# Hybrid retention and attention layer on one core: where four waits at stage borders sit, and an order written out by hand

## The chip, the cores and the metric

The kernel runs on one core of a Trainium2 chip. A core has five engines that run their own instruction queues side by side: TensorE (PE, matrix products into PSUM; PEld is its weight load), VectorE (DVE), ScalarE (ACT), GpSimd (POOL) and SyncE (SP, which here only issues DMAs). They wait for each other through semaphores. The metric is device microseconds of one execution; lower is better. A profiled execution gives the trace, with times counted from the start of its span.

## What is computed

One layer of a diffusion backbone, batch 1: 1024 latent tokens of width 1024 and 256 context tokens. All is fp32. Cut to what matters here:

```python
h_lat = rms_norm(x, norm1_g) * (1 + sc1) + sh1              # scale and shift from c @ w_mod
# one input projection: retention q, k, v, gate | attention q, k, v
(rq, rk, rv, rg), (dq, dk, dv) = split_heads(h_lat @ w_in, rope_r, rope_d)   # and the same for ctx
# retention, 4 heads, both directions, chunks of 128:
S = S * c_dec + einsum('jd,je->de', kc * k_dec, vc)         # state carried from chunk to chunk
o = (qc @ kc.T * intra) @ vc + (qc * q_dec) @ S
y_ret = silu(rg) * (group_norm(o_forward) + group_norm(o_backward))
# differential attention, 4 heads, 1024 queries, 1280 keys:
a = softmax(q1 @ k1.T) - lam * softmax(q2 @ k2.T)
y_diff = rms_norm(a @ v) * g
x = x + g1 * (concat(y_ret, y_diff) @ w_out)
# gated MLP with a depthwise convolution of width 3 along the tokens:
u = conv3(h2 @ w_up); a, b = split(u)
x = x + g2 * ((silu(a) * b) @ w_down);  out = rms_norm(x) * final_g
```

## The kernel before

**Products in three passes.** Every large product splits both operands into a high and a low part (a ScalarE copy makes the high, a VectorE subtraction the low) and adds three products of 128x512 in `passes` (L129 to L134). A block of 512 output columns for 128 rows is 24 such products.

**Stages.** Modulation and first norm; the seven column blocks of the input projection, streamed in four slices of 512 KB each by `stream_block` (L213); retention, whose steps are generators that `tick` (L387) advances by a rate for each contraction step of a projection that runs at the same time (`beside`, L393); attention; output projection; the MLP, whose products are combined by a Strassen-like scheme over blocks j of columns; the down projection with the last norm.

**Who sets the order.** A planner that simulates the engines orders each engine's instructions, from the order in which the code emits them, their dependencies and the reuse of memory by tile pools. `in_order(start, engines)` (L120) pins the instructions emitted since `start` to the emitted order on the named engines. SP and POOL queues are in order as planned: a DMA that has to wait holds all behind it.

**The retention states.** `states_before` (L326) is a generator. Its first step emits three loads `kvgb` (L232); its second emits the first state product `pub` (L347, L348). At L854 the slices of block 3 are loaded, and at L855 the generator is put beside the gate projection `pn` (L856) at 36 steps in 62 ticks; a tick is three products.

**From queries to attention.** The queries are projected by `transposed` (L466) in blocks (head, half) of 24 products `pl`; `rotated` (L438) turns each: ScalarE swaps quarters of 32 partitions into `xb` (four times L443), VectorE forms `xa` (L446, L447, L448), `split_store` makes `xhl` (L434, L435) and SP stores it to `dq` (L436). The last two blocks are emitted at L992, after the first eight operations of attention unit 0 (`EARLY`, L990).

An attention unit is 128 queries of one head, 32 in all. Its operations are named by letters (L66): S scores (two maps, six products each into three PSUM banks, L890), M least value (L893, VectorE), E exponential with its sum (L897, ScalarE), R and C the weighted difference of both maps (L901, L902, L905, VectorE), T and K transposes and their copies in three groups `aT` (L910, L916), V value products (L922), O, Q copy and square (with `e` on GpSimd, L933), f the factor (VectorE L936, GpSimd power L937, kept as `pool_ins`), n, Y, h, l the scaled and turned result. Each map has one PSUM tile, so S of the next unit waits for E of this one. The loop over n at L1031 emits them in the order of `TAU` and pins it at L1051. The tiles `aT` lie in memory that the rotation's tiles had before.

**The MLP's first blocks.** L1390 to L1435 are an order by hand, pinned on PE, DVE and ACT. `multiplied` (L1380) is a VectorE product and, for an even block, a difference (L1273). `seventh_out` (L1333) copies a PSUM bank on ScalarE and adds the bank `fifth` on VectorE (L1335); that bank is then used again by the product `third` (L1360).

**The end.** `finished(r)` (L1648) scales the right half of rows r on ScalarE, stores it from SP (L1650), and `scaled` (L1570) does the left half on VectorE and stores it from SP (L1573).

Of the kernel before, what the change touches and what calls it, by code (L numbers as in the profile page):

```python
# [8 lines left out]
F32 = mybir.dt.float32  # L9
F32R = mybir.dt.float32r  # L10
# [7 lines left out]
P = 128  # L18
# [43 lines left out]
SPARE = (16, 4)  # L62
MOD_TICKS = 7
FIRST_LOADS = (22, 23, 25, 26, 28, 30)
EARLY = ("S1", "M1", "S0", "M0", "E1", "E0", "R", "C")
# [5 lines left out]
def r32(ap):  # L71
    return ap.bitcast(F32)
# [3 lines left out]
def kernel(  # L76
# [52 lines left out]
    def passes(ps, lt, rt, first, last, more=False):  # L129
        lh, ll = lt  # L130
        rh, rl = rt
        mm(ps, lh, rh, start=first, stop=False, skip_group_check=more)  # L132
        mm(ps, lh, rl, start=False, stop=False, skip_group_check=more)  # L133
        mm(ps, ll, rh, start=False, stop=last, skip_group_check=more)  # L134
# [21 lines left out]
    with ExitStack() as p1:  # L156
# [169 lines left out]
        def states_before():  # L326
            seq = [(h, c) for h in range(H) for c in (1, 0) + tuple(range(9, 2, -1))]
            pairs = [(h, c // 2) for h, c in seq if c % 2]
            waiting = []

            def ask():
                if pairs:
                    waiting.append(load_kvg(*pairs.pop(0), "b", ROW_KB, 2, bufs=5))

            kv = ahead = prev = Sb = None
            for _ in range(3):
                ask()
            for h, c in seq + [(None, None)]:
                cur = ahead
                if c is not None:  # L340
                    if c % 2:
                        kv = waiting.pop(0)
                        ask()
                    ahead = h, c, kv[:, 0, c % 2, :], kv[:, 1, c % 2, :]
                if cur is not None:
                    hc, cc, kk, v = cur
                    pu = pst.tile([P, P], F32, name="pub", tag="tr")  # L347
                    mm(pu, kk, v, start=True, stop=True)  # L348
# [502 lines left out]
        rtx = p1.enter_context(ExitStack())  # L851
        sb = rtx.enter_context(tc.tile_pool(name="sb", bufs=H - 1, side="right", reuse_waits="tile"))
        rt = rtx.enter_context(tc.tile_pool(name="rt", bufs=2, side="right", reuse_waits="tile"))
        wg = stream_block(3)  # L854
        beside(states_before(), 36 / 62)  # L855
        natural(wg, lat_lhs, range(NT), store_to(kvg_row(ROW_G), func=AF.Silu, c0=NTC))  # L856
        wg = stream_block(6)
        beside(outputs(), 1.05, -12.0)
# [10 lines left out]
        def loads(name, bufs=1, **kw):  # L869
            return aload.enter_context(tc.tile_pool(name=name, bufs=bufs, side="right", reuse_waits="tile", **kw))  # L870

        aq0, ak0, av, aq1, al, ak1 = (loads(*args) for args in (("aq0",), ("ak0",), ("av", 2), ("aq1",), ("al", 2), ("ak1",)))
        pss = {m: loads(f"pss{m}", space=PSUM) for m in (1, 0)}
        n_units = NT * H
        units = {}

        class Unit:
            def __init__(self, i):
                self.h, self.qt = divmod(i, NT)
# [31 lines left out]

            def turned(self, g):
                if self.aT is None:
                    self.aT = at.tile([P, NKT, P], F32, name="aT")
                n = min(4, NKT - 4 * g)
                nc.scalar.copy(self.aT[:, 4 * g : 4 * g + n, :], self.pt[g][:, :n, :])  # L916

# [41 lines left out]
        def load(i):  # L959
            h, qt = divmod(i, NT)  # L960
            ms = ((1, 2), (0, 1)) if i == 0 else ((0, 2),)
            behind = iter(FIRST_LOADS if i == 0 else ())

            def spaced():
                n = next(behind, None)
                return nullcontext() if n is None else tc.issue_after(steps[n].pool_ins)
            if qt == 0:
                cur["k"] = (ak0, ak1)[h % 2].tile([P, 2, LK], F32R, name="ks")
# [16 lines left out]
        warm = al.tile([P, 64], F32, name="warm", bufs=1)  # L985
        nc.scalar.activation(warm[:, 0:1], nlam, AF.Exp)
        fore = [load(i) for i in range(3)]
        units[0] = Unit(0)
        vars(units[0]).update(fore[0])
        for op in EARLY:  # L990
            units[0].run(op)
        transposed(wg, dq_d, rtab, 32, -DIFF_SCALE, 0, by_head[-TAIL:])  # L992
        psl.close()

    ctx_ya = ctx.enter_context(ExitStack())
# [27 lines left out]


    with ExitStack() as p2:
        at = p2.enter_context(tc.tile_pool(name="at", bufs=2, reuse_waits="tile"))
        psa = p2.enter_context(tc.tile_pool(name="psa", bufs=1, space=PSUM, reuse_waits="tile"))

        start = len(nc.cur_bb.bb.instructions)
        order = sorted(TAU.items(), key=lambda it: it[1] % 1.0)  # L1030
        for n in range(n_units + 8):  # L1031
            if 0 < n < n_units:
                units[n] = Unit(n)
                vars(units[n]).update(fore[n])
            if n == 9:
                with tc.issue_after(units[n - 5].pool_ins.ins):
                    nc.gpsimd.dma_start(out=g1, in_=g1_d)
            if n in (8, 10, 12, 14):
                a, i = divmod(n // 2 - 4, 2)
                with tc.issue_after(units[n - 5].pool_ins.ins):  # L1040
                    nc.gpsimd.dma_start(out=yT[a][i][:, 0:H, :], in_=yr_d[i][:, a])
            for op, t in order:
                u = n - int(t)
                if 0 <= u < n_units and (u or op not in EARLY):
# [201 lines left out]
    with ExitStack() as p4:  # L1246
# [238 lines left out]
    with ExitStack() as p5:  # L1485
# [161 lines left out]

        def finished(r):  # L1648
            nc.scalar.activation(acc[r][:, C:], acc[r][:, C:], AF.Copy, scale=sm4[:, r, 0:1])
            nc.sync.dma_start(out=out[r * P : (r + 1) * P, C:], in_=acc[r][:, C:])  # L1650
            scaled(r, 0, C)

        for t in range(4):
# [87 lines left out]
```

## Time and profile before

| | us |
|---|---|
| median of 3 runs | 1395.55 (1393.97 to 1398.44) |
| the profiled execution | 1397.64 |
| its span, first to last instruction | 1395.9 |
| ScalarE, GpSimd busy | 740.3, 340.7 |
| mean granted TensorE clock | 0.996 |

Matrix products are pipelined: a 128x512 product is shown with 0.39 us, and the next one starts some 0.23 us after it, so a busy TensorE is not one at its peak. A row of the timeline has the start, the duration (of all merged instructions with x2, x6), engine, line, operation, out<-in tiles and, in brackets, the idle time before it and what ended it. PEclk of a window is the share of full clock that TensorE was granted.

### The profile page before, as it was taken

How to read it: one execution, taken by the hardware profiler on the slowest of the kernel's cores; microseconds unless marked ns; L12 is line 12 of the kernel's file. 1: busy time of each engine (PE TensorE's matmuls, PEld its weight loads, DVE VectorE, ACT ScalarE, POOL GpSimd, SP SyncE). 2: the span in 40 equal slices, each digit the busy share in tenths (PEclk: the TensorE clock that was granted, in tenths of full speed). 3: DMA queues.
4: the chain of work that ended last, by engine and by line, in shares of the span. 5: the costliest groups of instructions: out<-in, count | busy, mean ns of one | idle time of the engine just before them, and what ended most of it. 6: DMA issues, size and time to landing. Idle time of an engine off the chain costs nothing.

```text
span 1395.9 us, 19669 instructions
## 1 busy us (share of the span) xinstructions
PE 1368.6 (98%) x7028; PEld 1148.1 (82%) x7028; DVE 1019.3 (73%) x1516; ACT 740.3 (53%) x1414; POOL 340.7 (24%) x379
## 2 busy tenths in 40 slices
PE   8999999999999899999999999999999999999997
PEld 6788888788888799998888878888888888888886
DVE  5867856623467788886357999877788777998756
ACT  5545444313466789997026645555445555455533
POOL 1310001501446223411201244233332220033003
PEclk9999999999999999999999999999999999999999
DMA  9467877876678587732321223323223226953324
GB/s 383 156 212 243 310 259 247 264 240 183 192 218 230 152 189 165 134 86 76 131 83 61 91 106 113 114 92 113 105 107 113 86 81 216 392 190 102 132 99 151
DMA packets 107113, 230.88 MB, mean 165 GB/s; under 512 B 9540, under 2 KB 42820, under 8 KB 105096
## 3 DMA queue, kind: packets, MB, share of 16 engines
q1 hardware_dynamic: 98888, 204.73, 42.9%
q0 software_dynamic: 8128, 24.91, 8.1%
q8 instruction: 55, 0.90, 0.3%
q14 instruction: 42, 0.34, 0.1%
HBM read 165.37 MB, written 64.23 MB: 164 GB/s over the span
## 4 chain that ended last, share of the span: by engine, by line
PE 45%; DVE 3%; DMA 3%; issue 1%; SPq 0%; ACT 0%; POOLq 0%; DVEq 0%; POOL 0%; ACTq 0%
PE chain L133 5%; PE chain L132 5%; PE chain L134 5%; PE c L134 4%; PE c L133 4%; PE c L132 4%; PE third L132 2%; PE third L133 2%; PE third L134 2%; DMA W<-w_down 2%; PE po L134 2%; PE po L133 2%; PE po L132 2%; PE second L132 1%; PE second L134 1%; PE second L133 1%
## 5 line engine op out<-in xcount | busy, mean ns | idle before, releaser
L132 PE MATMUL pl<-hT,whi 128*128 128x512 f32 x256 | 107.5, 420 | 0.0
L132 PE MATMUL chain<-T,whi 128*128 128x512 f32 x264 | 102.8, 390 | 0.0
L133 PE MATMUL chain<-T,whi 128*128 128x512 f32 x264 | 102.7, 389 | 0.0
L134 PE MATMUL chain<-T,wlo 128*128 128x512 f32 x264 | 102.7, 389 | 0.0
L134 PE MATMUL pl<-hT,wlo 128*128 128x512 f32 x256 | 100.4, 392 | 0.0
L133 PE MATMUL pl<-hT,whi 128*128 128x512 f32 x256 | 100.2, 392 | 0.0
L893 DVE TENSOR_REDUCE mt<-pA 128x1 f32<-128x1280 f32 x64 | 95.4, 1490 | 5.1 <-PE pA L890 4.6
L890 PE MATMUL pA<-ks,qhl 128*128 128x512 f32 (+1 forms) x384 | 90.7, 372 | 3.3 <-ACT p L897 3.3
L443 ACT ACTIVATE xb<-pl 32x512 f32<-32x512 f32 (+1 forms) x96 | 56.7, 590 | 64.7 <-PE pl L134 44.6
L134 PE MATMUL c<-whi,ghl 128*128 128x512 f32 x232 | 90.4, 390 | 0.1
L132 PE MATMUL c<-whi,ghl 128*128 128x512 f32 x232 | 90.3, 389 | 0.0
L133 PE MATMUL c<-wlo,ghl 128*128 128x512 f32 x232 | 90.3, 389 | 0.0
L1212 POOL TENSOR_TENSOR cmb<-wrb 128x512 f32<-128x512 f32 x20 | 31.2, 1559 | 239.7 <-DMA wrb<-w_up 131.6
L897 ACT ACTIVATE p<-pA,mt 128x1280 f32<-128x1280 f32 x64 | 85.4, 1335 | 2.8 <-DVE mt L893 1.5
L132 PE MATMUL pn<-whi,hT 128*128 128x512 f32 x192 | 85.5, 445 | 0.0
L890 PEld LDWEIGHTS pA<-ks,qhl 128*128 128x128 f32 x384 | 68.4, 191 | 15.5 <-ACT p L897 4.1
L1063 ACT CAST whi<-cmb 128x512 fp32r<-128x512 f32 x62 | 38.5, 622 | 76.5 <-PE chain L133 63.4
L134 PE MATMUL pn<-whi,hT 128*128 128x512 f32 x192 | 76.3, 398 | 1.0 <-POOL hT L608 1.0
L922 PE MATMUL pv<-va,aT 128*128 128x128 f32 x640 | 76.9, 275 | 0.1
L133 PE MATMUL pn<-wlo,hT 128*128 128x512 f32 x192 | 75.9, 395 | 0.0
L922 PEld LDWEIGHTS pv<-va,aT 128*128 128x128 f32 x640 | 74.0, 192 | 0.7 <-DVE yT L951 0.3
L1064 DVE TENSOR_TENSOR wlo<-cmb,whi 128x512 fp32r<-128x512 f32 x62 | 58.0, 940 | 18.7 <-ACT whi L1063 18.7
(324 smaller groups left out, 3884.0 us busy)
## 6 DMA issues: line engine op xcount, KB each, us to landing
raw<-w_in SPq DMA_DIRECT2D x32, 512.0 KB, 5.6
wm<-w_mod SPq DMA_DIRECT2D x32, 512.0 KB, 4.6
wra<-w_up SPq DMA_DIRECT2D x24, 512.0 KB, 3.3
wrb<-w_up SPq DMA_DIRECT2D x23, 512.0 KB, 3.5
W<-w_down SPq DMA_DIRECT2D x44, 256.0 KB, 6.0
ad<-s SPq DMA_DIRECT2D x20, 512.0 KB, 3.1
wra<-ad SPq DMA_DIRECT2D x20, 512.0 KB, 3.3
wrb<-ad SPq DMA_DIRECT2D x18, 512.0 KB, 4.1
```

The lines of the kernel that those rows point to most:

```text
L132: mm(ps, lh, rh, start=first, stop=False, skip_group_check=more)
L133: mm(ps, lh, rl, start=False, stop=False, skip_group_check=more)
L134: mm(ps, ll, rh, start=False, stop=last, skip_group_check=more)
L443: nc.scalar.activation(xb[q * blk : (q + 1) * blk, :], pt[o : o + blk, :], AF.Copy, scale=scale)
L890: mm(self.pa[m][:, c0:c1], self.q[:, i, m, qs], self.k[:, m, c0:c1], start=(i == 0), stop=(i == 1))
L893: nc.vector.tensor_reduce(out=self.mt[:, m : m + 1], in_=self.pa[m][:, :LK], axis=AX.X, op=ALU.min)
L897: nc.scalar.activation(self.p[m], self.pa[m][:, :LK], AF.Exp, scale=-1.0, bias=self.mt[:, m : m + 1], accum_out=self.s[:, m : m + 1])
L922: mm(self.pv, self.aT[:, c, :], self.v[:, c, :], start=(c == 0), stop=(c == NKT - 1))
L1063: nc.scalar.copy(hi, src)
L1064: nc.vector.tensor_tensor(out=lo, in0=src, in1=r32(hi), op=ALU.subtract)
L1212: nc.gpsimd.tensor_tensor(out=s1, in0=b1, in1=b2, op=ALU.add)
```

## The change

1. `states_before` becomes a function that emits its three first loads at once and returns the generator `states_after`; it is called ahead of the slices of block 3. The rate becomes 36 steps in 58 ticks and the first due value -2.5.
2. `EARLY` and the `transposed` call for the last two query blocks go. In their place stands an order by hand, pinned on PE, DVE and ACT, that mixes the parts of the two blocks with the first operations of units 0, 1 and 2. The last block is only copied on ScalarE (`copied`); its quarters are swapped by four DMAs within SBUF and it is rotated and split by five GpSimd operations.
3. The fourth of these is made to follow unit 0's `pool_ins` on GpSimd.
4. Units 0 and 1 take `aT` from a pool of their own (`at0`), in the place where the key tiles of odd heads (`ak1`) were; `ak1` is opened at n = 5. A tile `gap` of 12.8 KB a partition pushes the other attention tiles away from the rotation's.
5. Block 2's `seventh_out` comes ahead of block 0's `multiplied`.
6. The last store of a right half (r = 7) is issued from ScalarE's queue.

```diff
@@ states
-            kv = ahead = prev = Sb = None
             for _ in range(3):
                 ask()
+            return states_after(seq, waiting, ask)
+        def states_after(seq, waiting, ask):
+            kv = ahead = prev = Sb = None
...
+        states = states_before()
         wg = stream_block(3)
-        beside(states_before(), 36 / 62)
+        beside(states, 36 / 58, -2.5)
@@ attention's pools and first operations
-        aq0, ak0, av, aq1, al, ak1 = (loads(*args) for args in (("aq0",), ("ak0",), ("av", 2), ("aq1",), ("al", 2), ("ak1",)))
+        aq0, ak0, av, aq1, al = (loads(*args) for args in (("aq0",), ("ak0",), ("av", 2), ("aq1",), ("al", 2)))
+        ak = [ak0]
+        first_aT = ExitStack()
+        at0 = first_aT.enter_context(tc.tile_pool(name="at0", bufs=2, side="right", reuse_waits="tile"))
...
-                    self.aT = at.tile([P, NKT, P], F32, name="aT")
+                    self.aT = (at if self.i > 1 else at0).tile([P, NKT, P], F32, name="aT")
...
-        for op in EARLY:
-            units[0].run(op)
-        transposed(wg, dq_d, rtab, 32, -DIFF_SCALE, 0, by_head[-TAIL:])
+        class LastQueries:
...
+            def copied(self):
+                nc.scalar.activation(self.xa, self.pt, AF.Copy, scale=-DIFF_SCALE)
+            def rotated_on_gpsimd(self):
+                for q in range(4):
+                    nc.sync.dma_start(out=self.xb[q * 32 : (q + 1) * 32, :], in_=self.xa[(q ^ 1) * 32 : ((q ^ 1) + 1) * 32, :])
+                self.hl = er.tile([P, 2, 512], F32R, name="xhl")
+                done = []
+                for o, a, b, op in (
+                    (self.xa, self.xa, self.cs, ALU.mult),
+                    (self.xb, self.xb, self.sn, ALU.mult),
+                    (self.hl[:, 0, :], self.xa, self.xb, ALU.add),
+                    (self.xa, self.xa, self.xb, ALU.add),
+                    (self.hl[:, 1, :], self.xa, r32(self.hl[:, 0, :]), ALU.subtract),
+                ):
+                    done.append(nc.gpsimd.tensor_tensor(out=o, in0=a, in1=b, op=op).ins)
+                return done[3]
+        begun = set()
+        start = len(nc.cur_bb.bb.instructions)
+        qa, qb = [LastQueries(*by_head[i]) for i in (-2, -1)]
+        begin(0, "S1", "M1", "E1")
+        qa.products(0, 4)
+        begin(0, "S0", "M0")
+        qa.products(4, KD)
+        begin(0, "E0")
+        qa.cosine()
+        qa.swapped()
+        begin(0, "R", "C")
+        qb.products(0, 2)
+        begin(1, "S1", "M1")
+        qa.sine()
+        begin(1, "E1")
+        qa.high()
+        qb.products(2, 4)
+        begin(1, "S0", "M0")
+        qa.low()
+        qa.store()
+        begin(1, "E0")
+        qb.products(4, 6)
+        begin(2, "S1", "M1")
+        qb.products(6, KD)
+        qb.copied()
+        begin(2, "E1", "S0")
+        in_order(start, FORCE[:3])
+        last_sum = qb.rotated_on_gpsimd()
+        qb.store()
@@ attention's loop
+        gap = p2.enter_context(tc.tile_pool(name="gap", bufs=1, reuse_waits="tile")).tile([P, 3200], F32, name="gap")
...
+            if n == 5:
+                first_aT.close()
+                ak.append(loads("ak1"))
...
         in_order(start)
+        tc.add_manual_dep(last_sum, units[0].pool_ins.ins.name, mybir.DependencyInfo(mybir.DependencyClass.NoSync, mybir.DependencyReason.DATA), reason="order")
@@ the MLP's first blocks
-        b0.multiplied()
         b2.fifth_new()
         b2.seventh()
         b2.seventh_out()
+        b0.multiplied()
@@ finished(r)
-            nc.sync.dma_start(out=out[r * P : (r + 1) * P, C:], in_=acc[r][:, C:])
+            (nc.scalar if r == 7 else nc.sync).dma_start(out=out[r * P : (r + 1) * P, C:], in_=acc[r][:, C:])
```

`products`, `cosine`, `swapped`, `sine`, `high`, `low` and `store` of `LastQueries` are the steps of `transposed`, `rotated` and `split_store`, one by one.

More of the change, by code (lines that the diff above doesn't have):

```diff
@@ L64 @@
 FIRST_LOADS = (22, 23, 25, 26, 28, 30)
-EARLY = ("S1", "M1", "S0", "M0", "E1", "E0", "R", "C")
 OPS = dict(S="scores", M="least", E="exp", R="ratio", C="combine", T="turn", K="turned", V="values", O="out", Q="square", f="rstd", n="norm", Y="final", h="high", l="low")
@@ L878, in __init__ @@
             def __init__(self, i):
+                self.i = i
                 self.h, self.qt = divmod(i, NT)
@@ L967, in load @@
             if qt == 0:
-                cur["k"] = (ak0, ak1)[h % 2].tile([P, 2, LK], F32R, name="ks")
+                cur["k"] = ak[h % 2].tile([P, 2, LK], F32R, name="ks")
             if qt % 4 == 0:
@@ L987, with begin, __init__, products @@
         fore = [load(i) for i in range(3)]
-        units[0] = Unit(0)
-        vars(units[0]).update(fore[0])
-        for op in EARLY:
-            units[0].run(op)
-        transposed(wg, dq_d, rtab, 32, -DIFF_SCALE, 0, by_head[-TAIL:])
+        for i in range(3):
+            units[i] = Unit(i)
+            vars(units[i]).update(fore[i])
+        def begin(i, *todo):
+            for op in todo:
+                units[i].run(op)
+                begun.add((i, op))
+        class LastQueries:
+            def __init__(self, h, hf):
+                self.h, self.hf = h, hf
+                self.pt = ps_a.tile([P, 512], F32, name="pl", tag="mm")
+                self.xa = er.tile([P, 512], F32, name="xa")
+                self.xb = er.tile([P, 512], F32, name="xb")
+                self.cs, self.sn = (rtab[:, i, hf * 512 : (hf + 1) * 512] for i in range(2))
+            def products(self, k0, k1):
+                h = self.h
+                for k in range(k0, k1):
+                    passes(self.pt, wg(k, h * P, (h + 1) * P), tuple(hT[a][self.hf][:, k, :] for a in range(2)), k == 0, k == KD - 1)
+            def swapped(self):
+                for q in range(4):
+                    nc.scalar.activation(self.xb[q * 32 : (q + 1) * 32, :], self.pt[(q ^ 1) * 32 : ((q ^ 1) + 1) * 32, :], AF.Copy, scale=-DIFF_SCALE)
+            def cosine(self):
+                nc.vector.scalar_tensor_tensor(out=self.xa, in0=self.pt, scalar=-DIFF_SCALE, in1=self.cs, op0=ALU.mult, op1=ALU.mult)
+            def sine(self):
+                nc.vector.tensor_tensor(out=self.xb, in0=self.xb, in1=self.sn, op=ALU.mult)
+                nc.vector.tensor_tensor(out=self.xa, in0=self.xa, in1=self.xb, op=ALU.add)
+            def high(self):
+                self.hl = er.tile([P, 2, 512], F32R, name="xhl")
+                nc.scalar.copy(self.hl[:, 0, :], self.xa)
+            def low(self):
+                nc.vector.tensor_tensor(out=self.hl[:, 1, :], in0=self.xa, in1=r32(self.hl[:, 0, :]), op=ALU.subtract)
+            def store(self):
+                c0 = self.hf * 512
+                nc.sync.dma_start(out=dq_d[self.h][:, :, :, c0 : c0 + 512].rearrange("m p a l -> (m p) a l"), in_=r32(self.hl))
+            def copied(self):
+                nc.scalar.activation(self.xa, self.pt, AF.Copy, scale=-DIFF_SCALE)
+            def rotated_on_gpsimd(self):
+                for q in range(4):
+                    nc.sync.dma_start(out=self.xb[q * 32 : (q + 1) * 32, :], in_=self.xa[(q ^ 1) * 32 : ((q ^ 1) + 1) * 32, :])
+                self.hl = er.tile([P, 2, 512], F32R, name="xhl")
+                done = []
[8 more added lines that the diff above has]
+                return done[3]
@@ L1031 @@
         for n in range(n_units + 8):
-            if 0 < n < n_units:
+            if 2 < n < n_units:
                 units[n] = Unit(n)
@@ L1043 @@
                 u = n - int(t)
-                if 0 <= u < n_units and (u or op not in EARLY):
+                if 0 <= u < n_units and (u, op) not in begun:
                     units[u].run(op)
```

## Prediction

> **What bounds the kernel now.** I read the page's shares of busy time first, then the waits of TensorE (line waiting, releaser: us in total, times, longest), then the windows around each wait that the change touches (us, busy time and count of PE, PEld, DVE, ACT, POOL, then granted clock, DMA share, GB/s).
>
> ```profile
> PE 1368.6 (98%) x7028; PEld 1148.1 (82%) x7028; DVE 1019.3 (73%) x1516; ACT 740.3 (53%) x1414; POOL 340.7 (24%) x379
> PE pA L890 <- ACT p L897: 3.3, 3, 1.9
> PE pub L348 <- DMA kvgb<-kvg: 2.1, 1, 2.1
> PE pt L910 <- ACT aT L916: 1.9, 2, 1.3
> PE third L132 <- DVE ub L1335: 1.8, 2, 1.4
> PE pyt L312 <- POOL y L308: 1.3, 1, 1.3
> ```
>
> TensorE is busy for 98% of a span of 1395.9 us, so only some 27 us can be had without removing products, and the change removes none. The four longest waits add up to 9.1 us, and each sits where one part of the change works. A wait can cost more than its length, though, because the clock falls behind it. The retention states come first.
>
> ```profile
> 268.29 0.39 PE L132 MATMUL pn<-whi,hT 128*128 128x512 f32 x1
> 268.71 2.71 SPq L232 DMA_DIRECT2D kvgb<-kvg  x5
> 270.78 0.39 PE L134 MATMUL pn<-whi,hT 128*128 128x512 f32 x1
> 273.29 0.80 PE L348 MATMUL pub<-kvgb 128*128 128x128 f32 x2 [2.13 <-DMA kvgb<-kvg]
> 271.00:273.30 2.30, 0.17 (x2) 0.01 (x1) 0.80 (x2) 0.03 (x1) 1.33 (x2) 0.97 1.00 281
> 273.30:276.60 3.30, 3.30 (x9) 2.72 (x10) 0.29 (x1) 0.00 (x0) 1.16 (x1) 0.51 0.88 302
> 276.60:281.00 4.40, 4.40 (x25) 3.76 (x24) 1.05 (x3) 1.53 (x2) 0.00 (x0) 1.00 0.90 291
> ```
>
> The three first loads of states_before are issued on SP only at 268.71. The twelve pn products of four ticks are over at 270.78 + 0.39, and the first pub product stands until 273.29. Then TensorE runs at a granted 0.51 for 3.3 us. The entry to attention is the second place.
>
> ```profile
> 457.97 1.28 ACT L986 ACT_TABLE_LOAD   x1
> 458.59 1.49 DVE L893 TENSOR_REDUCE mt<-pA 128x1 f32<-128x1280 f32 x1
> 462.29 0.59 ACT L443 ACTIVATE xb<-pl 32x512 f32<-32x512 f32 x1 [2.83 <-PE pl L134]
> 462.90 1.33 ACT L897 ACTIVATE p<-pA,mt 128x1280 f32<-128x1280 f32 x1
> 465.92 1.55 DVE L905 SCALAR_TENSOR_TENSOR p<-p,r,p 128x1280 f32<-128x1280 f32 x1
> 467.53 2.46 PE L890 MATMUL pA<-ks,qhl 128*128 128x512 f32 x12
> 471.87 1.44 PE L890 MATMUL pA<-ks,qhl 128*128 128x512 f32 x6 [1.87 <-ACT p L897]
> 477.24 0.58 ACT L916 COPY aT<-pt 128x512 f32<-128x512 f32 x1 [1.67 <-DMA dq<-xhl]
> 477.88 1.09 PE L910 MATMUL pt<-ident,p 128*128 128x128 f32 x4 [1.33 <-ACT aT L916]
> 479.19 2.41 PE L890 MATMUL pA<-ks,qhl 128*128 128x512 f32 x6 [0.23 <-ACT p L897]
> 481.88 2.40 PE L922 MATMUL pv<-va,aT 128*128 128x128 f32 x20
> 452.60:481.90 29.30, 23.44 (x108) 18.73 (x107) 21.11 (x29) 20.27 (x34) 5.57 (x11) 0.94 0.55 153
> ```
>
> From unit 0's first scores (452.6) to its first value product (481.9) TensorE is busy for 23.4 of 29.3 us. The cause stands on ScalarE: a swap of the next-to-last query block sits in its queue ahead of unit 0's exponentials and waits 2.83 us for products, so VectorE has next to nothing to do from the end of unit 0's two minima (458.59 + 2 x 1.5 = 461.6) to its C at 465.92. Later VectorE has to do everything at once, and TensorE waits 1.87 and 1.33 us among others. The six scores at 479.19 take 2.41 us, those at 471.87 took 1.44.
>
> **The states.** At the full clock a product starts every 0.227 us (twelve pn from 268.29 to 270.78 and the next start). From 270.78 to 276.60, when the full clock is back, seven pn and two pub pairs were done; at 0.227 a product, or a pair, that is 2.0 of 5.8 us, so **3.8 us** are lost: 2.1 of wait, the rest mostly clock. The edit issues the loads ahead of the slices of block 3, and it moves the second call of the generator from tick 4 to tick 8 ((2+2.5)/(36/58) = 7.25), twelve products or 2.7 us later. Even if the loads started only at 268.71, the first operand, there by 273.29, would be in time for a product due at 268.29 + 24 x 0.227 = 273.7. What is late next is the second pair of loads, 0.5 us behind and not needed before tick 10. If the three loads do go ahead, SP spends 1.6 us earlier (2.71/5 each) in front of slices that lie there long before use. Ends: 0 gained if SP blocks behind them, 3.8 gained if not; I take 3.8, since the later tick alone suffices.
>
> The Trainium skill ("TensorE: Matmul & The Clock Gate", What's actually happening) says that the clock falls after an idle window of about 3.4 us. Here it fell after 2.3 us, so the row decides; by the page's figure only 2.1 to 2.5 us would go here, and the sum below would be 1.3 to 1.7 us smaller.
>
> **The entry to attention.** The pinned order puts E1 and E0 of unit 0 ahead of the swaps, spreads the scores of units 0 to 2 between the 48 last query products, and moves the last block's rotation to GpSimd. I follow the queues with the rows' durations (scores 2.46/2 = 1.2, twelve products 2.7, M 1.5, E 1.33 and 0.1 behind it, C 1.55, a swap or another 512-wide step 0.6). TensorE: S1 of unit 0 ends at 455.3 (its wait of 1.3 for the last pyt stays, nothing touches it), twelve products to 458.1, S0 to 459.3, then products to 463.4. VectorE, free at 458.6 as before: M1, M0 to 461.6. ScalarE: E1, E0 to 463.2. S1 of unit 1 at 463.4 finds its PSUM free. Then cosine, R, C to 465.3; swaps to 465.6; M1 of unit 1 to 466.8, E1 to 468.4; S1 of unit 2 at 468.6 is just in time. sine to 468.0, M0 to 469.5, E0 to 471.0; S0 of unit 2 at 471.2, to 472.4. M1 of unit 2 to 471.6, the plain copy of the last block to 472.0, E1 of unit 2 to 473.4, K1 to 474.0: the third transpose group, due at 473.1, waits some 1.0 us for it. S1 of unit 3 to 475.9, T1 of unit 1 to 476.3, and the value product of unit 0 starts at 476.3, where before it started at 481.9: **5.5 us**. VectorE ends M1 of unit 3 at 477.6, the same 1.3 behind, so the loop starts in step, and the products behind it are as many as before. The 1.67 us on the dq store goes because at0 and the gap keep aT off the rotation's tiles.
>
> The rotation's five GpSimd steps and four copies within SBUF are new. Neither has a row here; the nearest are these.
>
> ```profile
> 252.21 0.68 DVE L447 TENSOR_TENSOR xb<-xb,rtab 128x512 f32<-128x512 f32 x1
> 247.03 1.19 DVE L447 TENSOR_TENSOR xb<-xb,rtab 128x512 f32<-128x512 f32 x1
> 259.65 2.52 POOL L428 TENSOR_TENSOR xq<-xa,qd 128x512 f32<-128x512 f32 x2 [1.41 <-DVE xa L448]
> 250.06 3.98 POOL L428 TENSOR_TENSOR xq<-xa,qd 128x512 f32<-128x512 f32 x2 [0.68 <-POOL xq L428]
> kvg<-st SPq DMA_DIRECT2D x32, 128.0 KB, 1.9
> 495.00:518.00 23.00, 23.00 (x175) 21.61 (x174) 20.53 (x27) 20.46 (x49) 6.21 (x14) 1.00 0.88 193
> ```
>
> A 512-wide step costs GpSimd 1.26 to 1.99 us, and beside such steps VectorE's L447 takes 1.19 for 0.68. So five steps are 6.3 to 10.0 us of GpSimd, and each can hold a C back by 0.5 to 2.0. VectorE is busy for 20.5 of 23 us in the loop, 0.6 free a unit, 1.8 over three units. I charge **0.5** of the ends 0 and 8.2 (five times 2.0, less 1.8), since C is the only long step of the loop with two SBUF inputs, a quarter of a unit. The result is needed in unit 28, far off. For unit 0 the square e stands behind three of the steps: 472.0 + 1.6 issue (4 x 0.41, as SP's last store below) + 1.9 landing + 3 x 1.5 = 480.0, and its factor is due at about 480.5. That is close, and a rival.
>
> **Block 2's sum and the last store.**
>
> ```profile
> 786.60:800.00 13.40, 13.40 (x61) 11.10 (x60) 13.16 (x14) 8.20 (x14) 8.71 (x5) 1.00 0.54 184
> 800.00:814.70 14.70, 13.42 (x59) 10.49 (x57) 14.66 (x15) 10.27 (x16) 7.44 (x5) 1.00 0.16 55
> 814.70:834.40 19.70, 19.33 (x84) 15.69 (x84) 19.66 (x21) 9.32 (x14) 8.11 (x5) 1.00 0.36 134
> 1391.11 0.72 ACT L1649 ACTIVATE acc<-acc,sm 128x512 f32<-128x512 f32 x1 [0.32 <-POOL sm L1568]
> 1391.85 0.33 SPq L1650 DMA_DIRECT2D out_dram<-acc  x1
> 1392.28 0.41 SPq L1573 DMA_DIRECT2D out_dram<-acc  x1
> ```
>
> The wait of 1.4 us at 814.8 goes, since L1335 no longer stands behind b0's product and difference (1.7 us). But VectorE is busy for 47.5 of the 47.8 us from 786.6 to 834.4, with the same steps in either order, and TensorE waits for its next L1335 at 834.5 already. It will arrive there 1.4 us sooner and wait 1.8 instead of 0.4. Ends: 1.4 gained if the next sum also comes sooner, 0.6 lost if the steps pushed back are wanted; I take **0**. At the end the right half's store no longer holds SP, so the left half's goes at about 1391.9 and not 1392.28: **0.4**, with ends 0 (a first store from ScalarE as slow as SP's two) and 0.4.
>
> **Sum.** 3.8 + 5.5 - 0.5 + 0 + 0.4 = 9.2 us: span 1386.7, and 1388.4 for the profiled execution, which took 1397.64 (1.7 outside the span). It lies 2.1 above the median of the runs, 1395.55, and within their spread of 4.5. For the median I forecast 1395.55 - 9.2 = **1386.4**.
>
> **Rivals.** (A) GpSimd and VectorE hold each other up at the entry, or e comes late: half of the 5.0 is given back, 1388.9 (up to 1391.3). For it: VectorE at 1.19 for 0.68, and 480.0 against 480.5. Against it: most of VectorE's work there reads PSUM. The Trainium skill ("SBUF — State Buffer", Who interferes with whom) says that a VectorE instruction with two SBUF inputs and a GpSimd one that reads SBUF shut each other out for the whole instruction; the rows above lean that way, since neither engine's time is unchanged. (B) The entry gives nothing: only states and store remain, 1395.55 - 4.2 = 1391.4; down to 1394 if the states fail too. For it: an order made by hand meets other data times, S0 of unit 0 needs a key load that took up to 7.6 us elsewhere, and VectorE was the busy engine (9.06 of 9.2 us from 470.0). Against it: VectorE's idle 4 us from 461.6 are used now. (C) Block 2's sum does bring its 1.4: 1385.0. (D) Slower: GpSimd's third step ends so late that VectorE stands at unit 0's factor and all minima queue behind it. This decides from 9.2 + 4.2 = 13.4 us of delay, a third step ending after about 494; the slowest landing of a state load (6.6 us) and 1.99 a step give only 486, so SP would have to hold the four copies some 8 us more. With 15 us it gives 1401.
>
> ```profile
> 470.00:479.20 9.20, 4.61 (x23) 3.42 (x23) 9.06 (x13) 6.00 (x11) 0.00 (x0) 0.93 0.29 113
> DMA to landing us min/median/max: 3.0/4.1/6.6
> DMA to landing us min/median/max: 4.0/6.4/7.6
> ```
>
> **How the numbers follow.** A measurement of this kernel tells about 0.3% (4.2 us) from no change. Forecast 0.49, A 0.20, C 0.06: faster 0.75. B 0.18: within 0.3%. D 0.07: slower. The low end takes the entry without any loss but the pyt wait (another 1.5), C's 1.4 and 1 us of spread: 1382.5. The high end holds A and the better part of B: 1392.5.
>
> **What would show it.** Right: no wait of pub on kvgb and a clock of 1.00 behind it; the first pv product 24 us after the first pA and not 29.3; ScalarE's exponentials of unit 0 ahead of the swaps; the wait at the next L1335 near 1.8 us; the last two stores issued within 0.1 us. Wrong: C or the factor of the first units waiting for GpSimd, a load of ks ending a wait of S0, or waits in the loop that were not there.

## The result, and the profile after

| | before | after |
|---|---|---|
| median of 4 runs, us | 1396.28 (1393.97 to 1398.44) | 1387.95 (1387.70 to 1388.11) |
| the profiled execution, its span | 1397.64, 1395.9 | 1388.11, 1386.3 |
| mean granted TensorE clock | 0.996 | 0.999 |

The ratio is 0.994, with a 95% interval of 0.9926 to 0.9953: 8.3 us less by the medians, where 9.2 were forecast. The spread fell from 4.5 to 0.4 us as well, which no step forecast; over nine runs (with e5 below) it is 1.2 us, and the experiments show where the rest came from.

Here are the shares of the page of the kernel after, and the waits of TensorE in it (line waiting, releaser: us in total, times, longest). The lines have moved: pub is now L350, pA L897, C L912, aT L923 and block 2's sum L1433.

```profile
PE 1365.4 (98%) x7028; PEld 1145.9 (83%) x7028; DVE 1018.0 (73%) x1512; ACT 738.6 (53%) x1410; POOL 346.4 (25%) x384
```

```profile
PE pt L917 <- ACT aT L923: 1.9, 3, 0.7
...
PE third L131 <- DVE ub L1433: 0.7, 1, 0.7
```

Of the four long waits of before, those of pA and pub are gone, that of third has shrunk from 1.8 to 0.7, and that of pt is 1.9 in total as before, though its longest is 0.7 and no longer 1.3. TensorE's busy time fell by 3.2 us though it does the same 7028 products, which goes with the higher clock. Where the lead is won and given back is seen from the starts of products in the tile view:

| | before | after | lead |
|---|---|---|---|
| last pub | 324.4 | 321.6 | 2.8 |
| first pA | 452.6 | 449.2 | 3.4 |
| first pv | 481.9 | 472.5 | 9.4 |
| last pv | 661.1 | 653.9 | 7.2 |
| first third | 777.6 | 769.5 | 8.1 |
| last third | 1176.2 | 1166.6 | 9.6 |
| end of the span | 1395.9 | 1386.3 | 9.6 |

The entry wins 6.0, attention gives back 2.2, the second norm's border brings 0.9, the MLP's first blocks 1.5. Next, the timeline of the kernel after at the states, SP and TensorE together, and then the windows there (us, then busy time and count of PE, PEld, DVE, ACT, POOL, then granted clock, DMA share, GB/s).

```profile
269.41 0.37 SPq L431 DMA_DIRECT2D rqk<-xq  x1
269.83 2.71 SPq L231 DMA_DIRECT2D kvgb<-kvg  x5
...
274.85 0.38 PE L350 MATMUL pub<-kvgb 128*128 128x128 f32 x2
```

```profile
271.00:274.90 3.90, 3.90 (x19) 3.24 (x18) 1.93 (x3) 1.16 (x1) 1.81 (x2) 1.00 1.02 293
449.20:472.50 23.30, 21.28 (x108) 17.56 (x107) 18.63 (x25) 17.53 (x29) 3.80 (x6) 1.00 0.65 180
```

The loads are not ahead at all: they go at 269.83, behind the same rqk store, where before they went at 268.71. The first pub is simply due later, and finds its data. The second row of the windows is the entry from the first pA to the first pv: 23.3 us where it was 29.3, at a clock of 1.00 where it was 0.94. The timeline of VectorE, GpSimd and TensorE shows what happens behind it:

```profile
473.90 1.25 DVE L909 SCALAR_TENSOR_TENSOR r<-r,sa,nlam 128x1 f32<-128x1 f32 x1
475.19 2.67 DVE L912 SCALAR_TENSOR_TENSOR p<-p,r,p 128x1280 f32<-128x1280 f32 x1
481.07 1.43 DVE L909 SCALAR_TENSOR_TENSOR r<-r,sa,nlam 128x1 f32<-128x1 f32 x1
...
473.88 1.26 POOL L1054 TENSOR_TENSOR xb<-xb,rtab 128x512 f32<-128x512 f32 x1
475.21 1.29 POOL L1054 TENSOR_TENSOR xhl<-xa,xb 128x512 fp32r<-128x512 f32 x1
...
481.17 1.30 POOL L1054 TENSOR_TENSOR xhl<-xa,xhl 128x512 fp32r<-128x512 f32 x1
...
478.46 2.40 PE L929 MATMUL pv<-va,aT 128*128 128x128 f32 x20
485.87 2.50 PE L929 MATMUL pv<-va,aT 128*128 128x128 f32 x20 [0.29 <-DVE yT L958]
491.73 2.40 PE L929 MATMUL pv<-va,aT 128*128 128x128 f32 x20
```

Three VectorE steps that lie beside a GpSimd step of the rotation take 1.25 for 0.22, 2.67 for 1.55 and 1.43 for 0.22 us (the short durations are those of the same lines a unit later). Value products then follow each other after 7.41 us (478.46 to 485.87) instead of the loop's 5.86 (to 491.73).

### The profile page after: what moved, and what is told of

Read it like the earlier page. It is cut to its first block, busy times and chain, and to the rows that moved or that the text cites. A ratio compares the mean times of both kernels' runs of the same rounds, so it can differ in the third digit from the quotient of the medians.

```text
span 1386.3 us, 19666 instructions
## 1 busy us (share of the span) xinstructions
PE 1365.4 (98%) x7028; PEld 1145.9 (83%) x7028; DVE 1018.0 (73%) x1512; ACT 738.6 (53%) x1410; POOL 346.4 (25%) x384
## 4 chain that ended last, share of the span: by engine, by line
PE 65%; DVE 1%; POOL 1%; issue 0%; ACT 0%; DMA 0%; SPq 0%; POOLq 0%; ACTq 0%; DVEq 0%
PE chain L131 6%; PE chain L132 6%; PE chain L133 6%; PE c L132 5%; PE c L133 5%; PE c L131 5%; PE pv L929 5%; PE pA L897 5%; PE third L131 3%; PE third L133 3%; PE third L132 3%; PE pt L917 2%; PE po L133 2%; PE po L132 2%; PE po L131 2%; PE second L131 1%
## 5 line engine op out<-in xcount | busy, mean ns | idle before, releaser
L897 PE MATMUL pA<-ks,qhl 128*128 128x512 f32 (+1 forms) x384 | 89.6, 368 | 0.0
L445 ACT ACTIVATE xb<-pl 32x512 f32<-32x512 f32 (+1 forms) x88 | 52.0, 591 | 61.6 <-PE pl L133 41.9
L897 PEld LDWEIGHTS pA<-ks,qhl 128*128 128x128 f32 x384 | 67.9, 189 | 11.5
```

The costliest lines, as they stand in the source:

```text
L445: nc.scalar.activation(xb[q * blk : (q + 1) * blk, :], pt[o : o + blk, :], AF.Copy, scale=scale)
L897: mm(self.pa[m][:, c0:c1], self.q[:, i, m, qs], self.k[:, m, c0:c1], start=(i == 0), stop=(i == 1))
```

## The experiments

In all of them the kernel before was run beside the others; its medians there were 1395.87 (28 runs, e1 to e4), 1395.42 (13, e5 to e8), 1395.96 (17, e9 to e11) and 1394.4 (9, e12).

### One part alone

e1: the later tick, without the loads ahead.

```diff
-        beside(states_before(), 36 / 62)
+        beside(states_before(), 36 / 58, -2.5)
```

> Only the rate 36/58 and the first due value -2.5 of the states; their three loads stay where they were. Theory (the later tick alone takes the wait away): no wait of pub on kvgb, a clock of 1.00 behind it, 3.8 us less than before. Rival (the loads had to go ahead): pub still waits some 2 us and the time moves by less than 1 us.

e2: the loads issued ahead in the code, at the old rate.

```diff
+        states = states_before()
         wg = stream_block(3)
-        beside(states_before(), 36 / 62)
+        beside(states, 36 / 62)
```

> Only the three loads emitted ahead of block 3's slices, at the old rate. Theory: the loads still start behind the store of the next-to-last rotation, near 269, the wait of 2.1 us and the 0.51 clock stay, 0 us gained (within 0.5). Rival: the loads start before 262 and 3.8 us go.

e3: the entry alone, that is the kernel after with parts 1, 5 and 6 undone.

> Only the pinned turn to attention with GpSimd's rotation, at0 and gap. Theory: the first value product comes 23.2 us after the first score product (29.3 before), some 2 us of this are given back by the third value product because VectorE's two-input steps wait for GpSimd, and about 4 us remain. Rival: the giving back belongs to the phase in which all parts together arrive, then 5.5 to 6 us remain.

e4: block 2's sum ahead, alone.

```diff
-        b0.multiplied()
         b2.fifth_new()
         b2.seventh()
         b2.seventh_out()
+        b0.multiplied()
```

> Only block 2's sum ahead of block 0's product. The prediction (VectorE is full, so the wait moves on to the next sum): 0 us, the next wait on ub grows from 0.4 to 1.8 us. Rival from the trace of after (the same VectorE steps take 1.5 us less there, since other ones fall beside GpSimd's sums): 1.0 to 1.6 us less, next wait near 0.7 us.

| | median, us | runs | ratio to before, 95% |
|---|---|---|---|
| e1 later tick | 1394.40 (1393.18 to 1397.78) | 11 | 0.9993 [0.9984, 1.0003] |
| e2 loads ahead | 1396.52 (1393.67 to 1399.12) | 11 | 1.0001 [0.9991, 1.0011] |
| e3 entry | 1391.07 (1390.15 to 1394.16) | 6 | 0.9968 [0.9955, 0.9980] |
| e4 sum ahead | 1395.70 (1393.05 to 1397.80) | 11 | 0.9998 [0.9989, 1.0007] |

The loads ahead do nothing: SP issues kvgb at the same place in its queue, and pub waits 1.6 us. The entry brings 4.8 us. The sum brings 0.2: its first wait is gone and the next one, 0.4 before, is 1.6, as the prediction said. The later tick takes the wait of pub away in the profile but brings 1.5 us by the medians and not 3.8, and its interval does not exclude that it brings nothing. Alone, the parts add up to some 6 us, 2 less than together.

### What the runs differ in: the clock

The kernels with the old entry spread over 3.5 to 6 us. The windows of TensorE tell why (us, busy time and count of PE, granted clock, DMA share, GB/s): first of the kernel before, then e4, then e1, then two windows of e2. In the first three, each window is set to begin where the clock changes, to within 0.1 us.

```profile
269.62:273.03 3.41, 1.55 (x7) 1.00 1.04 293
474.42:477.83 3.41, 1.43 (x6) 1.00 0.40 154
477.83:481.24 3.41, 3.13 (x9) 0.52 0.40 154
```

```profile
468.28:471.69 3.41, 1.54 (x9) 1.00 0.02 5
471.70:475.10 3.40, 2.76 (x11) 0.51 0.38 149
475.10:478.50 3.40, 2.93 (x10) 0.50 0.41 160
478.50:482.00 3.50, 3.50 (x15) 0.50 0.48 140
```

```profile
470.06:473.47 3.41, 1.81 (x10) 1.00 0.40 154
473.50:476.90 3.40, 2.35 (x7) 0.51 0.40 154
476.90:480.30 3.40, 3.40 (x15) 0.50 0.57 178
```

```profile
270.00:273.40 3.40, 1.75 (x9) 1.00 1.01 295
...
467.61:471.02 3.41, 1.70 (x10) 1.00 0.02 5
```

The clock is halved for a stretch of 3.41 us, or two or three of them, and each time TensorE was only about half busy in the 3.41 us ahead (1.43 to 1.81 us). In the kernel before the stretches at the states and at the entry begin at 273.03 and 477.83: 204.80 us apart, which is 60 times 3.41; and in all fourteen traces the full clock lasts for a whole multiple of 3.413 us between two changes. So the stretches lie on a fixed grid, and a stall costs what the grid makes of it: at the entry nothing in e2's profile, one stretch before, two in e1, three in e4. The stalls differ a little between these profiles as well, so that the grid alone decides is not shown. A window that is half busy does not always bring a stretch: in e2's profile one with 1.70 us of work at the entry brought none. At the states the length of the wait goes with it as well: the stretch came where pub waited longest (2.1 us before, 2.0 in e6 below) and not at waits of 1.6 to 1.8 us (e2, e3 and e4), which in e2 leave TensorE busy for 1.75 us of 3.40. The Trainium skill ("TensorE: Matmul & The Clock Gate", What's actually happening) says that the gate looks at free-running windows of 3.41 us, which fits; it says that the clock falls after an idle window, and here windows that were 42 to 53% busy could be enough. A half-clock stretch takes up to 1.7 us of work. With the new entry no profile has one there. The small spread needs the states' part too: the entry alone (e3) still spreads over 4.0 us.

### One part taken out of the changed kernel

Here the entry's chance is out of the way. e5 is the kernel after, once more.

> The changed kernel once more, beside the next three. Expected 1387.9 us within 0.3 us in every run, since its pauses of TensorE are too short to bring the half clock. If the small spread of its first four runs (0.4 us) was luck, runs up to 4 us longer will appear, as they do for the kernel before (1393.0 to 1398.8).

e6 has the states' part undone.

```diff
-        states = states_before()
         wg = stream_block(3)
-        beside(states, 36 / 58, -2.5)
+        beside(states_before(), 36 / 62)
```

> The changed kernel with the states' part undone. My theory: the wait of pub on kvgb (1.6 to 2.1 us in five profiles) comes back in every run and is not absorbed later, and in part of the runs a stretch of 3.41 us at half clock (1.7 us) comes with it: median 1.6 to 3.0 us above the changed kernel, and a spread of some 1.7 us or more. Rival, after the kernel with the later tick alone (0.9 to 1.5 us gained): most of the wait is absorbed behind it, 1 us. The prediction's term was 3.8.

e7 has the sum's part undone (`b0.multiplied()` ahead of `b2.fifth_new()` again).

> The changed kernel with block 2's sum behind block 0's product again. The prediction's step says 0 (the wait only moves to the next sum), and the sum alone gained 0.2 us. Rival: in the changed kernel's phase the sum ahead is worth what its trace gains on the one before between 786 and 825 us, so this kernel is 1.4 us slower, with third waiting for ub twice and 1.8 us in all.

| | median, us | runs | ratio to before, 95% |
|---|---|---|---|
| e5 after, again | 1388.44 (1387.49 to 1388.66) | 5 | 0.9945 [0.9933, 0.9958] |
| e6 without states | 1392.08 (1389.65 to 1393.11) | 9 | 0.9972 [0.9962, 0.9981] |
| e7 without sum | 1389.51 (1387.89 to 1390.08) | 5 | 0.9954 [0.9941, 0.9966] |

e5's runs spread over 1.2 us, more than the 0.3 either way that was expected and far less than 4. In this company the states are worth 3.6 us by the medians, above my 1.6 to 3.0 and close to the prediction's 3.8; by the fastest runs 2.2. The timeline of e6 has the wait, and its windows (all engines) the stretch behind it:

```profile
273.07 0.49 PE L350 MATMUL pub<-kvgb 128*128 128x128 f32 x2 [2.04 <-DMA kvgb<-kvg]
```

```profile
271.00:274.50 3.50, 1.46 (x8) 1.26 (x8) 0.98 (x2) 0.00 (x0) 2.50 (x2) 1.00 0.95 283
274.50:277.90 3.40, 3.40 (x11) 2.83 (x11) 0.69 (x2) 0.00 (x0) 0.00 (x0) 0.50 0.99 340
```

e6's four runs at a mean clock of 0.997 took 1392.4 to 1393.1, its others 1389.7 to 1392.1. The sum is worth 1.1 by the medians of five runs each, where alone it was worth 0.2, so neither the prediction's 0 nor the rival's 1.4 was right in both settings. Since e1 lay so far below e6's answer, it was run again as e11:

> The kernel before with the later tick alone, once more. My theory: the wait of 1.6 to 2.1 us is gone, but the entry's stall still brings 0 to 3 stretches of 3.41 us at half clock by chance, and block 2 can come in a slot that is 1.0 to 1.1 us worse, so the mean of its runs lies 1 to 2 us below that of before, and the spread stays at 4 us. If the states' 3.4 to 3.6 us of the changed kernel hold here too, the mean lies more than 2.8 us below.

Measured: 1395.09 (1393.34 to 1398.08, 12 runs), ratio 0.9996 [0.9986, 1.0005]. By the means that is 0.6 us, less than the 1 to 2 expected. So the later tick alone does bring only about 1 us, if that. Both its profiles, each of the slowest run of its set, have two half-clock stretches at the entry and 1.0 us of a wait that no other profile has; the timeline of e11:

```profile
787.84 1.30 POOL L1212 TENSOR_TENSOR cmb<-wrb 128x512 f32<-128x512 f32 x1 [30.63 <-DMA wrb<-w_up]
...
787.85 1.83 DVE L1064 TENSOR_TENSOR wlo<-cmb,whi 128x512 fp32r<-128x512 f32 x1
789.61 1.78 DVE L1064 TENSOR_TENSOR wlo<-wrb,whi 128x512 fp32r<-128x512 f32 x1
...
803.65 0.50 PE L134 MATMUL third<-yT,wlo 128*128 128x512 f32 x1 [1.02 <-DVE wlo L1064]
```

A GpSimd sum starts together with VectorE's subtraction for wlo, and both wlo take 1.8 us. That led to e12, below.

### GpSimd beside VectorE at the entry

e8: GpSimd's third and fourth step behind unit 0's power, the fifth behind unit 1's.

```diff
-        tc.add_manual_dep(last_sum, units[0].pool_ins.ins.name, ...)
+        for i, u in ((2, 0), (3, 0), (4, 1)):
+            tc.add_manual_dep(last_sum[i], units[u].pool_ins.ins.name, ...)
```

> The changed kernel with the third and fourth GpSimd step of the rotation behind unit 0's power and the fifth behind unit 1's. If GpSimd's steps beside VectorE's R and C cost the 2.1 us that the lead of the value products shrinks by after 472 us, then C of unit 1 (2.67 us) is back at 1.55, L909 of unit 2 (1.43) near 0.22, and 1.0 to 1.7 us are gained. If the lead shrinks for another reason, the time stays within 0.3 us.

Measured: 1386.92 (1386.70 to 1387.96, 5 runs), ratio 0.9938 [0.9925, 0.9952]: 1.5 us below e5. C takes 1.56 us where it took 2.67, but the two L909 still take 1.25 and 1.40, beside the second step and now the fourth. e9 goes further: the first step writes another tile and so need not wait for the swaps that read its input, and the fourth goes behind unit 1's power too.

```diff
-                    (self.xa, self.xa, self.cs, ALU.mult),
+                    (tmp, self.xa, self.cs, ALU.mult),
...
-        for i, u in ((2, 0), (3, 0), (4, 1)):
+        for i, u in ((2, 0), (3, 1), (4, 1)):
```

> The changed kernel with GpSimd's first step written to the other block's free tile, so that it need not wait for the swaps, and the third behind unit 0's power, the fourth and fifth behind unit 1's. If it is the pairing of a GpSimd step with a VectorE step of two SBUF inputs that costs time, both L909 (1.25 and 1.40 us in the kernel with later steps) come near 0.22 and the first pv products of units 1 and 2 come up to 1 and 2 us sooner than there: 1 to 2 us faster than that kernel's 1386.9. If L909 is long for another reason, its time and the kernel's stay.

Measured: 1386.66 (1385.05 to 1386.90, 5 runs), ratio 0.9933 [0.9919, 0.9946]. The timeline of e9:

```profile
468.37 1.55 DVE L912 SCALAR_TENSOR_TENSOR p<-p,r,p 128x1280 f32<-128x1280 f32 x1
...
473.79 0.22 DVE L909 SCALAR_TENSOR_TENSOR r<-r,sa,nlam 128x1 f32<-128x1 f32 x1
474.04 1.55 DVE L912 SCALAR_TENSOR_TENSOR p<-p,r,p 128x1280 f32<-128x1280 f32 x1
...
479.44 0.22 DVE L909 SCALAR_TENSOR_TENSOR r<-r,sa,nlam 128x1 f32<-128x1 f32 x1
...
468.52 2.53 POOL L1054 TENSOR_TENSOR xa<-xa,rtab 128x512 f32<-128x512 f32 x1 [11.93 <-ACT xa L1040]
472.53 1.27 POOL L1054 TENSOR_TENSOR xb<-xb,rtab 128x512 f32<-128x512 f32 x1 [1.47 <-DMA xb<-xa]
476.61 1.29 POOL L1054 TENSOR_TENSOR xhl<-xa,xb 128x512 fp32r<-128x512 f32 x1
...
478.01 2.40 PE L929 MATMUL pv<-va,aT 128*128 128x128 f32 x20
483.76 2.40 PE L929 MATMUL pv<-va,aT 128*128 128x128 f32 x20
489.53 2.40 PE L929 MATMUL pv<-va,aT 128*128 128x128 f32 x20
```

The first of the five GpSimd steps begins just behind unit 0's C (468.37) and is itself held, 2.53 us for 1.27. The other four lie beside VectorE's minima. Of VectorE's steps here only a later L909 is held, 0.44 us at 485.19; the two L909 above are at 0.22, and the value products follow after 5.75 and 5.77 us. From the first pA to the last pv it takes 202.5 us (449.1 to 651.6), in the kernel after 204.7 (449.2 to 653.9). So the meeting cost the changed kernel some 2.2 us. Of these the median gained 1.8 against e5 (1388.44 to 1386.66), and 1.6 against e10, the changed kernel but for its last store, which ran beside e9. Against e8 it gained 0.3, where 1 to 2 us were expected, though the value products end 0.8 us sooner after the first pA than in e8's profile.

### The last store

e10: the kernel after with its last store back on SP.

> The changed kernel with the last store back on SP. The prediction's term says 0.4 us slower than the changed kernel. The trace after says 0.25 us faster in the tail: from VectorE's last step to the end of the span 5.0 us (1381.26 to 1386.3) become 4.8, as before (1391.11 to 1395.9). The median may hide this, since block 2 alone moves runs by 1.1 us; the tail of the profile decides.

Measured: 1388.27 (1387.45 to 1389.55, 6 runs), ratio 0.9950 [0.9936, 0.9963]. The tails in the timelines, first of the kernel after, then of e10:

```profile
1381.26 0.75 DVE L1670 SCALAR_TENSOR_TENSOR acc<-acc,sm,fg 128x512 f32<-128x512 f32 x1 [1.08 <-POOL sm L1666]
...
1382.01 0.40 ACTq L1748 DMA_DIRECT2D out_dram<-acc  x1
...
1381.39 0.98 SPq L1671 DMA_DIRECT2D out_dram<-acc  x2
```

```profile
1380.70 0.75 DVE L1670 SCALAR_TENSOR_TENSOR acc<-acc,sm,fg 128x512 f32<-128x512 f32 x1 [1.08 <-POOL sm L1666]
...
1381.87 0.41 SPq L1671 DMA_DIRECT2D out_dram<-acc  x1
```

From VectorE's last step to the end of the span it takes 5.0 us in both (1386.3 and 1385.7), so neither the prediction's 0.4 nor my later 0.25 was there. The last issue ends 1.15 us after that step's start with ScalarE's queue (1382.41) and 1.58 after it with SP alone (1382.28), yet the data are there no sooner: what the earlier issue wins, the landing loses. The other profiles with ScalarE's store show 5.0 to 5.1 as well. With SP's store it is 5.0 in e3, which has the new entry, but 4.8 in the five profiles with the old one, so it is not the store that makes the difference to before; what does was not found.

### Two levels in the MLP's first blocks

Nine runs of the kernel after lie between 1387.5 and 1388.7, and behind the first third its two profiles differ in one place. The timelines of e5 (1388.66 us) and then of the kernel after (1388.11):

```profile
779.53 1.59 POOL L1310 TENSOR_TENSOR cmb<-wrb 128x512 f32<-128x512 f32 x1 [30.68 <-DMA wrb<-w_up]
...
779.89 1.78 DVE L1162 TENSOR_TENSOR wlo<-wrb,whi 128x512 fp32r<-128x512 f32 x1
...
825.33 0.50 PE L131 MATMUL third<-yT,whi 128*128 128x512 f32 x1 [1.57 <-DVE ub L1433]
```

```profile
780.86 1.53 POOL L1310 TENSOR_TENSOR cmb<-wrb 128x512 f32<-128x512 f32 x1 [31.37 <-DMA wrb<-w_up]
...
780.55 0.69 DVE L1162 TENSOR_TENSOR wlo<-wrb,whi 128x512 fp32r<-128x512 f32 x1
...
824.88 0.50 PE L131 MATMUL third<-yT,whi 128*128 128x512 f32 x1 [0.75 <-DVE ub L1433]
```

GpSimd's first sum starts when its weights land. If that is ahead of VectorE's wlo, wlo takes 1.78 us, VectorE, which is full here, stays 1.1 us late, and third waits 1.57 us and not 0.75. The profiles bear this out: from the first third to VectorE's last step it takes 611.4 to 611.7 us in the four with a short wlo (after, e8, e9 and e12 below), and 612.6 to 612.9 in e5, e6 and e10, where wlo is long. In e7, where wlo is long as well, it takes 613.0, so beside a long wlo the sum's place is worth only 0.1 to 0.5 us. The meeting alone does not sort the runs, though: e10 had the long wlo and took 1387.45 us, less than any of the nine, because it was 1.4 us ahead of the kernel after at the first third already. So after's is not among the three fastest profiles, as the expectation below has it. e12 is e9 with this sum held until that wlo is done, by a GpSimd step of one column that reads it:

```diff
+        lo4 = b1.halves["p4"][1]
...
-        b2 = Block(2)
+        b2 = Block(2, lo4)
...
+            nc.gpsimd.tensor_tensor(out=s1[:, 0, 0:1], in0=r32(behind[:, 0, 0:1]), in1=r32(behind[:, 0, 0:1]), op=ALU.add)
         nc.gpsimd.tensor_tensor(out=s1, in0=b1, in1=b2, op=ALU.add)
```

> The kernel with GpSimd's first step early, and one more edit: block 2's first GpSimd sum (cmb from wrb) comes behind VectorE's wlo of block 1's fourth part, by a GpSimd step of one column that reads that wlo. In ten of thirteen profiles the sum began before or on that wlo, which then took 1.78 us for 0.68, and third waited longer for ub; in the three fastest it began 0.15 to 0.3 us after its start. If this meeting is the cause of the two levels of the runs (1.1 us apart), wlo takes 0.68 in the profile, the later wait of third for ub is 0.8 or less, and the runs lie together at the lower level, 1385 to 1386 us, median 0.6 to 1.1 below 1386.7. If the sum's late start is only a sign of something else, the runs keep both levels or move up, since GpSimd now starts later.

Measured: 1385.11 (1384.41 to 1385.99, 5 runs), ratio 0.9931 [0.9917, 0.9945]. The timeline of e12:

```profile
777.13 0.69 DVE L1163 TENSOR_TENSOR wlo<-wrb,whi 128x512 fp32r<-128x512 f32 x1
...
778.16 2.26 POOL L1313 TENSOR_TENSOR cmb<-wrb 128x512 f32<-128x512 f32 x1
...
821.31 0.50 PE L131 MATMUL third<-yT,whi 128*128 128x512 f32 x1 [0.60 <-DVE ub L1436]
```

wlo takes 0.69, third waits 0.60, and no run lies above 1386.0, where three of e9's five lay above 1386.6. GpSimd starting later, and taking 2.26 us for the sum, cost nothing. That the runs gained by it is not shown: e9's profile had the short wlo too, the kernel before also ran 1.6 us lower beside e12 than beside e9 (1394.4 and 1395.96), the two ratios to it are alike (0.9931 and 0.9933), and of the 1.3 us between the two spans 1.2 are there at the first third, ahead of the edit. e12 has the lowest times of this study, about 3 us below the changed kernel by the medians and about 2 by the ratios.

## Why the prediction was right, and where it was off

**States (3.8).** The mechanism was right in its second half: the later tick alone takes the wait away (e1), and the loads ahead do nothing (e2), so it was well not to count on them. The size held in company (3.6), in part by luck, since it is not one fixed price: the wait is 1.6 to 2.1 us, and the half clock behind it, which I took for its fixed companion, came in two of the five profiles that have the wait (before and e6, whose waits are the longest, not e2, e3 and e4). Alone the part brought about 1 us, not clear of noise. At the first pA e1's profile is 3.5 us ahead of that of before (449.1 and 452.6), so the part works there too; behind it the lead is lost to the stretches at the old entry and to GpSimd in the MLP. Why GpSimd's sum starts just there in both e1 and e11 was not found. Since both profiles are of the slowest run of their set, what a median run loses is not known, and the gap between 3.6 and some 1 stays open.

**Entry (5.5, less 0.5).** The order came out as followed through the queues: 23.2 us from the first pA (449.24) to the first pv (472.47), against 23.7 forecast. The wait at the third transpose group is 0.74 (forecast 1.0). The step that was off is the charge of **0.5 for GpSimd and VectorE**: it measured 2.2. I reasoned that C is the only long VectorE step of the loop with two SBUF inputs, and left out the short ones. L909 works on 128x1 elements, takes 0.22 us, and was held for 1.0 and 1.2 us by a GpSimd step beside it: what counts is not the length of the VectorE step but that of the GpSimd step which it meets. The rule of the Trainium skill ("SBUF — State Buffer", Who interferes with whom) cited for rival A, that the two shut each other out for the whole instruction, fits the lengths in all three rows, and e9, where the minima that read PSUM lie beside such steps at their usual 1.5 us, fits it from the other side. Which of the two came first can't be read from the rows: in two of the three VectorE's step is shown as starting 0.02 and 0.10 us ahead of the GpSimd step that it seems to wait for. That the part alone was worth 4.8 against the 5.0 of the sum is partly luck: 6.0 were won at the entry, 2.2 given back, and some 0.9 came at the border of the second norm, which no step had.

**Block 2's sum (0).** Right for the kernel on its own (0.2: the wait moved, 1.6 for a forecast of 1.8), wrong for the changed one (1.1 by the medians; the next wait is 0.7 in the profile after and 1.6 in e5's). The order of VectorE's steps is the same in either; what I had not seen is that the meeting of GpSimd's sums with VectorE's steps decides how long VectorE's "full" stretch is, and that its phase shifts.

**Last store (0.4).** It lay at the end 0 of its bounds: issued earlier, landed no earlier.

**Sum and rivals.** 9.2 forecast, 8.3 measured, with the time 1.6 above the forecast and inside the range. Part of this closeness is luck, since errors cancel: GpSimd took 1.7 more than charged and the store brought none of its 0.4, while by the table of leads the second norm's border and the MLP's first blocks brought 2.4 that no term held. Rival A's mechanism was at work with 2.2 us instead of its 2.5, and C waiting for GpSimd was one of the signs named for being wrong; e was not late (the factor of unit 0 goes at 477.9, ahead of the 480.5 foreseen). Rival B fell with e3, rival D with GpSimd's third step ending at 476.5. Rival C came true in company only, with 1.1 of its 1.4.

## What to carry to other kernels

A stall of TensorE has a price in clock that changes from run to run: read several runs' spans and granted clocks before taking one profile's half-clock stretch as the cost, and expect a smaller spread as part of the gain. When work is handed to GpSimd, lay its steps beside VectorE steps that read PSUM, and look at the short two-input steps too, since each may wait out a whole GpSimd step. A part's worth measured alone need not be its worth in company: undo it from the finished kernel as well. And kernels that were run at different times are compared by their ratios to one that ran beside each, since that one moves too.

## What was not expected of the hardware

The half-clock stretches came in lengths of 3.4, 6.8 and 10.2 us, began 60 times 3.41 us apart within one run, and followed 3.41 us in which TensorE was busy for 1.43 to 1.81; yet 1.70 in e2 brought none. A VectorE step of one column took 1.25 and 1.43 us for 0.22 beside a GpSimd step of 1.26 to 1.30. Whether a GpSimd sum began 0.4 us ahead of a VectorE step of 0.68 us or 0.3 behind its start made that step 1.78 or 0.69 us long.
